# Stick-breaking attention with two keys to a scan step and a second projection with paired DMA transpositions

## Chip, cores and metric

The kernel runs on one core of one Trainium2 chip. The metric is the device time of one execution in microseconds (us); of several executions the median is taken. TensorE (PE in the profile) multiplies matrices, VectorE (DVE), ScalarE (ACT) and GpSimd (POOL) work element by element, SyncE (SP) issues most of the transfers.

## What is computed

Two transformer layers over 2048 tokens of width 1024. The change touches two pieces of the second layer. The first is the stick-breaking attention (4 heads of width 64, worked as 2 units of two heads), the second is the output projection with its residual and norm, which hands its rows to the feed-forward part.

```python
def stick_breaking_attention(q, k, v, g):
    ...
        z = jnp.einsum('bqhd,bkhd->bhqk', qb, kb).astype(jnp.float32) * scale
        mask = jnp.arange(end)[None, :] < (start + jnp.arange(Q_BLOCK))[:, None]
        log_1mb = jnp.where(mask, jax.nn.log_sigmoid(-z), 0.0)
        suffix = lax.cumsum(log_1mb, axis=3, reverse=True) - log_1mb
        a = jnp.where(mask, jnp.exp(jax.nn.log_sigmoid(z) + suffix), 0.0)
        outs.append(jnp.einsum('bhqk,bkhd->bqhd', a.astype(vb.dtype), vb))
    ...
    # second_block
        x = x + jnp.einsum('bse,ed->bsd', mix, w_out[l])
        h2 = rmsnorm(x, norm2_g[l])
        gate = jnp.einsum('bsd,df->bsf', h2, w_gate[l])
        up = jnp.einsum('bsd,df->bsf', h2, w_up[l])
        x = x + jnp.einsum('bsf,fd->bsd', jax.nn.silu(gate) * up, w_down[l])
```

## The kernel before

The program is built by a scheduler that sets the order on each engine by its own estimate, within what the data allow; each engine then works its list strictly in that order. Every f32 operand of a large product is kept as a sum of two f16 parts, a high part (a cast on ACT) and a low part (the difference, on POOL or DVE).

The span falls into five stretches: the first layer (0 to about 985 us), the attention of the second layer (`block2`, about 985 to 1950), its output projection (`out2`, overlapped with the end of the attention, to about 2110), the first half of the feed-forward part (`ffn_in`, to about 2970) and its second half (`ffn_out`).

`block2` works six units in turn; two of them are stick-breaking units (`stick`, from about 990 and from about 1456 us), four are differential-attention units (`diff`). The q, k, v projections of the following work (`unit_gemm`, tile `pg`) are mixed between the rows of a unit. In a stick unit each of 16 query blocks i has (i + 1) * 128 keys and two heads r; a row of keys is cut in pieces of at most 1024, the last keys first. That makes 48 pieces and 34,816 keys per partition and unit. A piece (`piece`, L1012) goes:

- scores on PE into PSUM (tile `sc`, four banks, L892 to L895);
- one minus beta as a sigmoid on ACT, PSUM to SBUF tile `e` (`g` in the code, six buffers, L1016);
- for the diagonal block beta itself, a second sigmoid on ACT, in place in PSUM (L1019);
- on DVE the running product over the keys from the last to the first, one key a step, in place (L1021), started from the first key of the piece before it (`carry`);
- on DVE the product of the last 127 keys with beta, read from PSUM (L1025);
- in `parts` the f16 high part on ACT (L907), the low part on POOL (L910), then one DMA transposition on SP (L912);
- some pieces later the sum over the values on PE (L922, L923).

The value rows are replaced by differences of neighbouring rows beforehand, so that the running product itself, and beta in the diagonal block alone, stand in for the attention weights. The delay between a piece and its parts is set by `self.pipe`: its split comes one piece later, its sum three more.

`out2` runs eight steps `u` of two token tiles each: load y and the residual x1 (SP), 48 matmuls per tile into `pq` (L665 to L667), add to the residual on DVE (L668), sum of squares on ACT into a junk PSUM bank (L670), store of x to `x2d` from SP (L671), the norm on DVE (L674, which overwrites x and so waits for that store), sums for a Strassen-like scheme (`seven`), high and low parts (L681, L682), and the DMA transpositions of those parts into the seven tiles `T7` (L693). The parts of one step are four of high and four of low; the low ones lie across the pairs in `T7`, so three of them take two transpositions each: eleven in a step. All of SP's transfers are issued in one list.

Of the kernel before, what the change touches and what calls it, by code (L numbers as in the profile page):

```python
# [7 lines left out]
F32 = mybir.dt.float32  # L8
# [3 lines left out]
AF = mybir.ActivationFunctionType  # L12
ALU = mybir.AluOpType
AX = mybir.AxisListType
PSUM = bass.MemoryType.PSUM
# [25 lines left out]
UN = (3, 6, 4, 4)  # L41
LAST_B = 2
PIPE = 2
UNITS = (0, 2, 3, 1, 4, 5)
MIX_ROWS = (0, 2)
FF = 2816
# [20 lines left out]
class Kernel:  # L67
# [556 lines left out]
    def out2(self, cw):  # L624

        nc, a = self.nc, self.a
        sm = self.pool("usm", 4, ctx=cw)  # L630
        gen = self.pool("gen", 3, ctx=cw)
        yp = self.pool("uy", 8, ctx=cw)
        m = self.pool("um", 5, ctx=cw)
        hp = self.pool("uh", 5, ctx=cw)
        sp = self.pool("us", 1, ctx=cw)
        pq = self.banks("upq", UPQ, cw)
        jp = self.pool("ujk", 1, PSUM, ctx=cw)
        w = [self.row_weight(a["wo2"], k, None if k < 5 else gen) for k in range(KD)]
        self.x2d = [self.dram.tile([128, 2, D], F32, name=f"x2d{t}") for t in range(8)]
        slots = [(self.x7, "x7")] * 6 + [(self.tp, "th")] * 4 + [(self.tp, "tl")] * 4  # L640
        self.T7 = [
            [pool.tile([128, 4, 2, 512], F16, tag=tag, name=tag) for pool, tag in slots[7 * h:7 * h + 7]]
            for h in range(2)
        ]
        gr = self.bcast(self.ws, a["n2"], D, "ws")
        for u in range(4 * NB // 2):
            half, tp = u // 4, u % 4
            xs = []
            for q in range(2):
                y = []  # L650
                for p in range(2):
                    t = yp.tile([128, KD, 128], F16, tag="y", name="y")
                    nc.sync.dma_start(t, self.y2d[2 * half + q][p][:, tp])
                    y.append(t)
                yh, yl = y
                r = m.tile([128, 2, 512], F32, tag="x2", name="x2")
                rf = r.rearrange("p h n -> p (h n)")
                nc.sync.dma_start(rf, self.x1d[8 * half + 4 * q + tp])
                ss = sm.tile([128, 2], F32, tag="ss", name="ss")
                for n in range(2):  # L660
                    ns = slice(n * 512, (n + 1) * 512)
                    ps = pq()
                    for k in range(KD):
                        wh, wl = w[k]
                        nc.tensor.matmul(ps, yh[:, k], wh[:, ns], start=k == 0, stop=False)  # L665
                        nc.tensor.matmul(ps, yh[:, k], wl[:, ns], start=False, stop=False)
                        nc.tensor.matmul(ps, yl[:, k], wh[:, ns], start=False, stop=k == KD - 1)  # L667
                    nc.vector.tensor_tensor(r[:, n], r[:, n], ps, ALU.add)  # L668
                    junk = jp.tile([128, 512], F32, tag="junk", name="junk")
                    nc.scalar.activation(junk, r[:, n], AF.Square, accum_out=ss[:, n:n + 1])  # L670
                nc.sync.dma_start(self.x2d[u][:, q], rf)  # L671
                nc.gpsimd.tensor_tensor(ss[:, 0:1], ss[:, 0:1], ss[:, 1:2], ALU.add)
                self.rstd(ss[:, 0:1], ss[:, 0:1], self.eps_rms, 1.0 / D)
                nc.vector.scalar_tensor_tensor(rf, rf, ss[:, 0:1], gr, ALU.mult, ALU.mult)  # L674
                xs.append(r)
            s3 = sp.tile([128, 3, 512], F32, tag="s3", name="s3")
            self.seven(xs[0], xs[1], *[s3[:, j] for j in range(3)], nc.vector)
            for j, src in enumerate((xs[0], xs[1], s3[:, 0:2], s3[:, 2:3])):
                n = src.shape[1]
                hl = [hp.tile([128, 2, 512], F16, tag="hl", name="hl")[:, 0:n] for _ in range(2)]  # L680
                nc.scalar.copy(hl[0], src)  # L681
                nc.vector.tensor_tensor(hl[1], src, hl[0], ALU.subtract)  # L682
                for p in range(2):
                    i = 7 * p + 2 * j
                    if n == 2 and i % 2 == 0:
                        spots = [(self.T7[half][i // 2][:, tp], hl[p])]
                    else:
                        spots = [
                            (self.T7[half][(i + x) // 2][:, tp, (i + x) % 2:(i + x) % 2 + 1], hl[p][:, x:x + 1])
                            for x in range(n)  # L690
                        ]
                    for to, of in spots:
                        nc.sync.dma_start_transpose(  # L693
                            to.rearrange("p x (k t) -> p (x k) t", t=128), of.rearrange("p x n -> p (x n)")
                        )

    def seven(self, r1, r2, s1, s2, s4, eng=None):

# [7 lines left out]
    def block2(self):  # L706
        self.y2d = self.y_scratch("y2d")
        with ExitStack() as c2:
# [3 lines left out]
            self.yp = self.pool("ayp", 1, ctx=c2)  # L712
            self.one = self.pool("aone", 1, ctx=c2)
            self.sm = self.pool("asm", 4, ctx=c2)
            self.pg = self.pool("pg", PGN, PSUM, ctx=c2)
            self.sc = self.pool("sc", SCN, PSUM, ctx=c2)
            self.po = self.pool("apo", PON, PSUM, ctx=c2)
# [2 lines left out]
            units += [("diff", 2 + h, 2 + h, 6 + h, 10 + h) for h in range(4)]  # L720
            units = [units[j] for j in UNITS]
            gemms = [self.unit_gemm(w, kind == "sb") for kind, _, *w in units]
            self.turn = self.turn2 = 0
            self.pipe, self.mixed = [], []
            self.later = []
            made = [0] * len(units) + [3 * NB]
            due = 0
# [276 lines left out]
    def stick(self, ops, k, b):  # L1004

        nc = self.nc
        rows = {}  # L1010

        def piece(i, r, p0, n, carry):  # L1012
            g = self.etile(0)
            own = None
            for ps, p, w in reversed(self.scores(ops, r, i, True, p0, p0 + n)):
                nc.scalar.activation(g[:, p - p0:p - p0 + w], ps[:, 0:w], AF.Sigmoid, scale=-1.0)  # L1016
                if p + w == (i + 1) * 128:
                    own = ps[:, w - 128:w - 1]
                    nc.scalar.activation(own, own, AF.Sigmoid)  # L1019
            rev = g[:, 0:n][:, ::-1]  # L1020
            nc.vector.tensor_tensor_scan(  # L1021
                rev, rev, self.zero.to_broadcast([128, n]), 1.0 if carry is None else carry, ALU.mult, ALU.add
            )
            if own is not None:
                nc.vector.tensor_tensor(g[:, n - 127:n], g[:, n - 127:n], own, ALU.mult)  # L1025

            def split():
                t = self.parts([(g[:, 0:n], 0, n)], g, self.etile(1), n, nc.gpsimd, True)
                self.pipe.append((PIPE, lambda: sum_up(t)))

            def sum_up(t):
                c = i % 4
                if r == 0 and carry is None:
                    rows[i] = self.po.tile([128, 2, 128], F32, tag="po", name="po")
                    if c == 0:
                        rows["o8"] = self.m.tile([128, 4, 2, 128], F32, tag="o4", name="o8")
                cols = slice(r * 64, (r + 1) * 64)
                self.spread(
                    [(t, p0 // 128, n // 128)], ops, cols, rows[i][:, :, cols], i, carry is None, p0 == 0
                )  # L1040
                if r == 1 and p0 == 0:
                    nc.vector.tensor_copy(rows["o8"][:, c], rows[i])
                    if c == 3:
                        ended()

            self.pipe.append((1, split))
            return g[:, 0:1] if p0 else None

        def ended():
            o4 = self.summed(rows["o8"])  # L1050

            def done():
                self.head_norm(o4, 64)
                self.finish(o4, k, b, self.col("sg"))

            self.later.append((LAST_DELAY if self.last_unit else DELAY, done))

        for c in range(4):
            i = b * 4 + c
            W = (i + 1) * 128  # L1060
            for r in range(2):
                carry = None
                for p0 in reversed(range(0, W, PIECE)):
                    carry = piece(i, r, p0, min(PIECE, W - p0), carry)
                    self.step()
            yield
        if b == NB - 1:
            while self.pipe:
                self.step()
# [44 lines left out]
        self.store(self.y2d, ct, b, ps, self.col("pscale", ct))  # L1114

    def part(self, half, p, q):
        i = 7 * p + q
        return self.T7[half][i // 2][:, :, i % 2]

    def ffn(self):  # L1120

# [315 lines left out]
```

## Time and profile before

| what | value |
|---|---|
| median of 3 runs | 3392.9 us (3389.72 to 3398.15) |
| profiled execution, its own time | 3387.5 us |
| its span, first to last instruction | 3385.7 us |
| PE busy | 3114.2 us (92%) |
| DVE busy | 2209.4 us (65%) |
| POOL busy | 1419.8 us (42%) |
| ACT busy | 1241.9 us (37%) |
| mean granted clock of PE | 0.967 of full speed |

The profile gives each engine's busy time, its instructions by source line with the operand names (out<-in), and the idle time of an engine with what ended it. A DVE or POOL duration includes time in which the instruction waits inside the engine. Busy times by stretch show which engine sets the pace where.

### The profile page before, as it was taken

How to read it: one execution, taken by the hardware profiler on the slowest of the kernel's cores; microseconds unless marked ns; L12 is line 12 of the kernel's file. 1: busy time of each engine (PE TensorE's matmuls, PEld its weight loads, DVE VectorE, ACT ScalarE, POOL GpSimd, SP SyncE). 2: the span in 40 equal slices, each digit the busy share in tenths (PEclk: the TensorE clock that was granted, in tenths of full speed). 3: DMA queues.
4: the chain of work that ended last, by engine and by line, in shares of the span. 5: the costliest groups of instructions: out<-in, count | busy, mean ns of one | idle time of the engine just before them, and what ended most of it. 6: DMA issues, size and time to landing. Idle time of an engine off the chain costs nothing. (4 is left out here: it accounts for less than half of the span.)

```text
span 3385.7 us, 46832 instructions
## 1 busy us (share of the span) xinstructions
PE 3114.2 (92%) x17736; PEld 1584.8 (47%) x17736; DVE 2209.4 (65%) x3573; ACT 1241.9 (37%) x2371; POOL 1419.8 (42%) x1155
## 2 busy tenths in 40 slices
PE   8999998999987798987798898899999999999998
PEld 4454454785434454544445443344444444334443
DVE  6986979624658886678856754456555655754437
ACT  5233232322136565565546632323222332311103
POOL 5344344413348644368734421333222233344324
PEclk9999999999989899999899999999999999999999
DMA  5101021214767764577556778322222222454334
GB/s 191 33 21 48 13 51 44 55 48 148 198 154 143 144 130 94 121 138 139 107 111 125 185 177 194 105 81 69 97 69 69 84 81 81 170 184 135 111 101 168
DMA packets 605570, 373.93 MB, mean 110 GB/s; under 512 B 508320, under 2 KB 549024, under 8 KB 604320
## 3 DMA queue, kind: packets, MB, share of 16 engines
q1 hardware_dynamic: 560192, 338.78, 39.1%
q10 hardware_dynamic: 45152, 32.17, 3.3%
q8 instruction: 139, 2.28, 0.3%
q14 instruction: 87, 0.71, 0.1%
HBM read 162.70 MB, written 82.31 MB: 72 GB/s over the span
## 5 line engine op out<-in xcount | busy, mean ns | idle before, releaser
L144 PE MATMUL pg<-th,w 128*128 128x512 f16 x1344 | 518.1, 386 | 24.8 <-DVE r L592 10.3
L146 PE MATMUL pg<-th,w 128*128 128x512 f16 x1344 | 519.7, 387 | 6.4 <-POOL w L123 3.2
L145 PE MATMUL pg<-tl,w 128*128 128x512 f16 x1344 | 519.2, 386 | 0.7 <-DVE tl L183 0.7
L910 POOL TENSOR_TENSOR e<-e 128x1024 f16<-128x1024 f32 (+7 forms) x192 | 366.7, 1925 | 231.2 <-ACT e L907 189.8
L1021 DVE TENSOR_TENSOR_SCAN e<-e,few 128x128 f32<-128x128 f32 (+7 forms) x96 | 223.7, 2347 | 36.1 <-ACT e L1016 24.0
L892 PE MATMUL sc<-k,q 128*128 128x512 f16 (+3 forms) x480 | 173.4, 364 | 63.1 <-DVE e L1025 44.2
L922 PE MATMUL po<-v,e 128*128 128x256 f16 (+1 forms) x1024 | 165.5, 264 | 66.5 <-DMA e<-e 62.8
L1161 POOL TENSOR_TENSOR w<-ws,w 128x1024 f16<-128x1024 f32 x20 | 48.6, 2431 | 393.2 <-ACT w L1160 393.2
L144 PEld LDWEIGHTS <-w 128*128 128x128 f16 x1344 | 133.6, 99 | 167.8 <-ACT w L122 13.7
L907 ACT CAST e<-e 128x1024 f16<-128x1024 f32 (+7 forms) x192 | 150.6, 794 | 167.1 <-DVE e L968 53.4
L145 PEld LDWEIGHTS <-w 128*128 128x128 f16 x1344 | 133.6, 99 | 166.6 <-issue 27.3
L146 PEld LDWEIGHTS <-w 128*128 128x128 f16 x1344 | 133.5, 99 | 163.8 <-issue 11.6
L1193 PEld LDWEIGHTS <-w 128*128 128x128 f16 x1232 | 121.1, 98 | 172.3 <-issue 32.6
L953 ACT ACTIVATE e<-e,nm 128x1024 f32<-128x1024 f32 (+4 forms) x192 | 171.2, 892 | 67.1 <-DVE e L948 50.0
L467 DVE SCALAR_TENSOR_TENSOR acc<-h,cols,acc 128x512 f32<-128x512 f32 x240 | 193.3, 825 | 2.4
L1192 PEld LDWEIGHTS <-w 128*128 128x128 f16 x1232 | 121.2, 98 | 155.7 <-ACT w L1160 8.7
L1194 PEld LDWEIGHTS <-w 128*128 128x128 f16 x1232 | 121.2, 98 | 150.3 <-issue 3.9
L893 PE MATMUL sc<-k,q 128*128 128x512 f16 (+3 forms) x480 | 172.8, 364 | 0.0
L123 POOL TENSOR_TENSOR w<-ws,w 128x1024 f16<-128x1024 f32 x52 | 117.7, 2266 | 125.2 <-ACT w L122 125.2
L922 PEld LDWEIGHTS <-e 128*128 128x128 f16 x1088 | 109.8, 105 | 108.2 <-DMA e<-e 75.2
L923 PE MATMUL po<-v,e 128*128 128x128 f16 (+1 forms) x1024 | 157.9, 218 | 0.0
L948 DVE TENSOR_SCALAR_CACHE_REDUCE e<-sc,nm 128x512 f32<-128x512 f32 (+3 forms) x192 | 123.0, 647 | 32.4 <-PE sc L893 12.9
(327 smaller groups left out, 7861.6 us busy)
## 6 DMA issues: line engine op xcount, KB each, us to landing
mid<-md SPq DMA_DIRECT2D x88, 448.0 KB, 4.2
ws<-in_w SPq DMA_DIRECT2D x48, 512.0 KB, 3.7
md<-mid SPq DMA_DIRECT2D x44, 512.0 KB, 3.4
md<-mid SPq DMA_DIRECT2D x22, 768.0 KB, 5.3
q<-qn SPq DMA_DIRECT2D x96, 128.0 KB, 2.6
ws<-in_wg SPq DMA_DIRECT2D x22, 512.0 KB, 3.5
ws<-in_wu SPq DMA_DIRECT2D x22, 512.0 KB, 4.1
ws<-in_wd SPq DMA_DIRECT2D x22, 512.0 KB, 4.3
```

Of the source, the lines that this page charges most:

```text
L144: nc.tensor.matmul(ps, wh[:, k], th[:, k], start=k == 0, stop=False)
L145: nc.tensor.matmul(ps, wh[:, k], tl[:, k], start=False, stop=False)
L146: nc.tensor.matmul(ps, wl[:, k], th[:, k], start=False, stop=k == KD - 1)
L467: nc.vector.scalar_tensor_tensor(acc[:, ct], src, wcol, acc[:, ct], ALU.mult, ALU.add)
L892: nc.tensor.matmul(ps[:, 0:n], q[:, 0], kk, start=True, stop=False)
L893: nc.tensor.matmul(ps[:, 0:n], q[:, 1], kk, start=False, stop=not last)
L907: cast = nc.scalar.copy(fv[:, o:o + w], src)
L910: eng.tensor_tensor(fv[:, n + o:n + o + w], src, fv[:, o:o + w], ALU.subtract)
L922: nc.tensor.matmul(po, t[:, 0, j], v, start=first and x == 0, stop=False)
L923: nc.tensor.matmul(po[:, 0], t[:, 1, j], v[:, 0], start=False, stop=last and x == len(todo) - 1)
L953: nc.scalar.activation(e[r][:, 0:n], e[r][:, 0:n], AF.Exp, bias=nm[:, len(sc) - 1:len(sc)], scale=-1.0, accum_out=ss[:, r, x:x + 1])
L1021: nc.vector.tensor_tensor_scan(rev, rev, self.zero.to_broadcast([128, n]), 1.0 if carry is None else carry, ALU.mult, ALU.add)
```

## The change

In a stick unit a scan step takes two keys: the recurrence multiplies by the odd and by the even key and writes the even position; the odd positions are then multiplied by their neighbour in a separate DVE instruction of half the piece. A piece that continues another first copies the carry behind its last key. Beta of the diagonal block goes to SBUF (tile `own`, three buffers), and its product moves to GpSimd. The low part of every third piece is made on VectorE. In `out2` the low parts get their own pairs of `T7` slots, so that each part is one transposition, eight in a step; the store to `x2d` is issued from ScalarE; the junk bank is taken from the other end of PSUM.

```diff
+LO_SHARE = 3
...
-        jp = self.pool("ujk", 1, PSUM, ctx=cw)
+        jp = self.pool("ujk", 1, PSUM, ctx=cw, side="right")
...
-                nc.sync.dma_start(self.x2d[u][:, q], rf)
+                nc.scalar.dma_start(self.x2d[u][:, q], rf)
...
                 for p in range(2):
-                    i = 7 * p + 2 * j
-                    if n == 2 and i % 2 == 0:
-                        spots = [(self.T7[half][i // 2][:, tp], hl[p])]
-                    else:
-                        spots = [
-                            (self.T7[half][(i + x) // 2][:, tp, (i + x) % 2:(i + x) % 2 + 1], hl[p][:, x:x + 1])
-                            for x in range(n)
-                        ]
-                    for to, of in spots:
-                        nc.sync.dma_start_transpose(
-                            to.rearrange("p x (k t) -> p (x k) t", t=128), of.rearrange("p x n -> p (x n)")
-                        )
+                    at = self.spot(p, 2 * j)
+                    nc.sync.dma_start_transpose(
+                        self.T7[half][at // 2][:, tp, at % 2:at % 2 + n].rearrange("p x (k t) -> p (x k) t", t=128),
+                        hl[p].rearrange("p x n -> p (x n)"),
+                    )
+
+    def spot(self, p, q):
+
+        return q if p == 0 else 8 + q if q < 6 else 7
...
+            self.bp = self.pool("abp", 3, ctx=c2)
...
                 if p + w == (i + 1) * 128:
-                    own = ps[:, w - 128:w - 1]
-                    nc.scalar.activation(own, own, AF.Sigmoid)
-            rev = g[:, 0:n][:, ::-1]
+                    own = self.bp.tile([128, 127], F32, tag="own", name="own")
+                    nc.scalar.activation(own, ps[:, w - 128:w - 1], AF.Sigmoid)
+            if carry is not None:
+                nc.vector.tensor_copy(g[:, n:n + 1], carry)
+            even, odd = [g[:, 0:n].rearrange("p (j x) -> p j x", x=2)[:, :, x] for x in range(2)]
             nc.vector.tensor_tensor_scan(
-                rev, rev, self.zero.to_broadcast([128, n]), 1.0 if carry is None else carry, ALU.mult, ALU.add
+                even[:, ::-1], odd[:, ::-1], even[:, ::-1], 1.0 if carry is None else carry, ALU.mult, ALU.mult
             )
+            w = n // 2 - (carry is None)
+            after = g[:, 2:n + 2].rearrange("p (j x) -> p j x", x=2)[:, 0:w, 0]
+            nc.vector.tensor_tensor(odd[:, 0:w], odd[:, 0:w], after, ALU.mult)
             if own is not None:
-                nc.vector.tensor_tensor(g[:, n - 127:n], g[:, n - 127:n], own, ALU.mult)
+                nc.gpsimd.tensor_tensor(g[:, n - 127:n], g[:, n - 127:n], own, ALU.mult)
+
+            self.pieces += 1
+            eng = nc.gpsimd if self.pieces % LO_SHARE else nc.vector
 
             def split():
-                t = self.parts([(g[:, 0:n], 0, n)], g, self.etile(1), n, nc.gpsimd, True)
+                t = self.parts([(g[:, 0:n], 0, n)], g, self.etile(1), n, eng, True)
...
     def part(self, half, p, q):
-        i = 7 * p + q
-        return self.T7[half][i // 2][:, :, i % 2]
+        at = self.spot(p, q)
+        return self.T7[half][at // 2][:, :, at % 2]
```

The scheduler moves instructions with it. On POOL, in the first stick unit at query block 12, the list before has low parts alone (the numbers are tile names; two pieces of each head alternate):

```order
L910 TENSOR_TENSOR e_10120<-e_10010,e_10120 128x1024
L910 TENSOR_TENSOR e_10150<-e_10098,e_10150 128x640
L910 TENSOR_TENSOR e_10175<-e_10124,e_10175 128x1024
L910 TENSOR_TENSOR e_10207<-e_10154,e_10207 128x640
L985 TENSOR_TENSOR o8_9689<-o8_9689 128x4x128
```

and after the change, at the same block, the products with beta (L1030) between them, and two of the low parts gone to DVE:

```order
L1030 TENSOR_TENSOR e_10165<-e_10165,own_10174 128x127
L909 TENSOR_TENSOR e_10189<-e_10075,e_10189 128x1024
L1030 TENSOR_TENSOR e_10225<-e_10225,own_10234 128x127
L909 TENSOR_TENSOR e_10248<-e_10193,e_10248 128x1024
L909 TENSOR_TENSOR e_10282<-e_10225,e_10282 128x640
L984 TENSOR_TENSOR o8_9734<-o8_9734 128x4x128
```

The product of the following diagonal piece (e_10225) now stands ahead of the low part of the piece before it (e_10193). On ACT at the same place after the change (L1016 and L1019 the sigmoids, L906 the casts):

```order
L1016 ACTIVATE e_10193<-sc_10197 128x512
L1016 ACTIVATE e_10225<-sc_10226 128x512
L1016 ACTIVATE e_10225<-sc_10229 128x128
L1019 ACTIVATE own_10234<-sc_10229 128x127
L1016 ACTIVATE e_10252<-sc_10253 128x512
L906 CAST e_10248<-e_10193 128x1024
L1016 ACTIVATE e_10252<-sc_10256 128x512
L906 CAST e_10282<-e_10225 128x640
```

A piece's cast stands behind the sigmoids of the next piece and ahead of those of the one after it, as it did before the change; what is new is that the cast of a diagonal piece (e_10225) now waits for POOL's product and not for DVE's.

On SP, in `out2`, step 6 of eight had these rows before (L671 stores to x2d):

```order
L671 DMA x2d6_18883<-x2_19981 128x1024
L693 DMA_TRANSPOSE th_18892<-hl_20050 128x8x128
L693 DMA_TRANSPOSE tl_18895<-hl_20051 128x4x128
L693 DMA_TRANSPOSE tl_18896<-hl_20051 128x4x128
L693 DMA_TRANSPOSE th_18893<-hl_20057 128x8x128
L693 DMA_TRANSPOSE th_18894<-hl_20064 128x8x128
L693 DMA_TRANSPOSE tl_18896<-hl_20058 128x4x128
L693 DMA_TRANSPOSE tl_18897<-hl_20058 128x4x128
L693 DMA_TRANSPOSE tl_18897<-hl_20065 128x4x128
L693 DMA_TRANSPOSE tl_18898<-hl_20065 128x4x128
L693 DMA_TRANSPOSE tl_18895<-hl_20071 128x4x128
L693 DMA_TRANSPOSE tl_18898<-hl_20072 128x4x128
```

and has these after it:

```order
L686 DMA_TRANSPOSE th_19088<-hl_20228 128x8x128
L686 DMA_TRANSPOSE tl_19092<-hl_20229 128x8x128
L659 DMA x2_20324<-x1d15_7508 128x1024
L686 DMA_TRANSPOSE th_19089<-hl_20234 128x8x128
L686 DMA_TRANSPOSE th_19090<-hl_20240 128x8x128
L686 DMA_TRANSPOSE tl_19093<-hl_20235 128x8x128
L686 DMA_TRANSPOSE tl_19094<-hl_20241 128x8x128
L686 DMA_TRANSPOSE tl_19091<-hl_20246 128x4x128
L686 DMA_TRANSPOSE tl_19091<-hl_20247 128x4x128
```

The three split pairs are whole, and the stores have left the list: they now stand in ACT's, right behind the second sum of squares of their tile.

## Rows read from the trace of the kernel before

**Rows 1.** The page's first part: busy us, share of the span and instructions by engine.

```profile
PE 3114.2 (92%) x17736; PEld 1584.8 (47%) x17736; DVE 2209.4 (65%) x3573; ACT 1241.9 (37%) x2371; POOL 1419.8 (42%) x1155
```

**Rows 2.** Busy us by stretch: both stick units, then two pieces of out2 and its end.

```profile
core 0: us, PE busy (x) PEld busy (x) DVE busy (x) ACT busy (x) POOL busy (x), PEclk, DMA share, GB/s
990.00:1169.00 179.00, 139.47 (x1026) 74.98 (x1025) 143.96 (x122) 101.38 (x237) 133.49 (x66) 0.93 0.72 141
1456.00:1642.00 186.00, 143.69 (x1038) 80.91 (x1037) 150.90 (x131) 109.84 (x251) 153.32 (x75) 0.88 0.72 134
...
2000.00:2050.00 50.00, 40.89 (x181) 17.63 (x178) 26.03 (x31) 13.83 (x25) 6.31 (x12) 0.92 0.89 227
2100.00:2140.00 40.00, 23.05 (x76) 8.19 (x75) 24.74 (x27) 15.02 (x22) 9.43 (x10) 0.79 0.66 155
```

**Rows 3.** DVE in order of time, first stick unit: start us, duration us, instruction [idle before].

```profile
992.77 0.42 DVE L1021 TENSOR_TENSOR_SCAN e<-e,few 128x128 f32<-128x128 f32 x1 [2.32 <-ACT e L1016]
...
1157.35 0.29 DVE L1025 TENSOR_TENSOR e<-e,sc 128x127 f32<-128x127 f32 x1
1157.56 2.35 DVE L1021 TENSOR_TENSOR_SCAN e<-e,few 128x1024 f32<-128x1024 f32 x1
...
1161.61 2.36 DVE L1021 TENSOR_TENSOR_SCAN e<-e,few 128x1024 f32<-128x1024 f32 x1 [1.71 <-issue]
...
1164.08 3.96 DVE L1021 TENSOR_TENSOR_SCAN e<-e,few 128x1024 f32<-128x1024 f32 x1
...
1168.80 0.14 DVE L962 COPY s<-ss 128x1 f32<-128x1 f32 x1
```

**Rows 4.** POOL in order of time, first stick unit.

```profile
995.55 0.43 POOL L910 TENSOR_TENSOR e<-e 128x128 f16<-128x128 f32 x1 [3.09 <-ACT e L907]
...
1111.36 2.12 POOL L910 TENSOR_TENSOR e<-e 128x1024 f16<-128x1024 f32 x1 [3.35 <-ACT e L907]
...
1158.85 7.04 POOL L910 TENSOR_TENSOR e<-e 128x1024 f16<-128x1024 f32 x2 [3.78 <-issue]
```

**Rows 5.** Waits in the second stick unit: us in total, times, longest.

```profile
PE sc L892 <- DVE e L1025: 29.1, 12, 5.1
...
ACT e L1016 <- PE po L923: 16.4, 11, 2.9
```

**Rows 6.** DVE in order of time at the end of out2.

```profile
2099.32 1.23 DVE L682 TENSOR_TENSOR hl<-x,hl 128x1024 f16<-128x1024 f32 x1 [1.11 <-ACT hl L681]
...
2118.37 2.50 DVE L674 SCALAR_TENSOR_TENSOR x<-x,ss,ws 128x1024 f32<-128x1024 f32 x2 [7.15 <-DMA x2d<-x]
```

**Rows 7.** First layer, line L385, 128 elements: runs of four or more (nt), single elements (f); min/median/max ns.

```profile
L385 DVE TENSOR_TENSOR Q<-Q,nt x96: 273/282/2211, 41.9 to 641.6; 128x128 f32<-128x128 f32 x96
L385 DVE TENSOR_TENSOR Q<-Q,f x48: 374/614/2343, 33.1 to 626.5; 128x128 f32<-128x128 f32 x48
```

**Rows 8.** SP's list in out2 by line, min/median/max ns; a third of the transpositions.

```profile
L693 SPq DMA_TRANSPOSE x<-hl x36: 1205/1258/2130, 1967.1 to 2040.6; - x36
...
L671 SPq DMA_DIRECT2D x2d<-x x16: 319/532/867, 1928.9 to 2116.0; - x16
```

**Rows 9.** PE in order of time in out2 and after: the matmuls with idle time before them.

```profile
2009.85 0.39 PE L665 MATMUL pq<-w,y 128*128 128x512 f16 x1 [2.08 <-DMA y<-y2d2h]
...
2051.45 0.61 PE L665 MATMUL pq<-w,y 128*128 128x512 f16 x1 [8.44 <-DMA y<-y2d3h]
...
2112.08 0.58 PE L1192 MATMUL pa<-x,w 128*128 128x512 f16 x1 [6.61 <-ACT junk L670]
2121.27 0.58 PE L1192 MATMUL pa<-x,w 128*128 128x512 f16 x1 [3.98 <-ACT s L1207]
2129.18 0.61 PE L1192 MATMUL pc<-x,w 128*128 128x512 f16 x1 [3.88 <-ACT w L1160]
```

**Rows 10.** SP in order of time at the end of out2.

```profile
2115.30 1.05 SPq L671 DMA_DIRECT2D x2d<-x  x2
...
2122.08 0.53 SPq L1148 DMA_DIRECT2D ws<-in_wg  x1
```

More of the change, by code (lines that the diff above doesn't have):

```diff
@@ L723, in block2 @@
             self.turn = self.turn2 = 0
-            self.pipe, self.mixed = [], []
+            self.pipe, self.mixed, self.pieces = [], [], 0
             self.later = []
```

## Prediction

> **What bounds the kernel now.** Read the page's busy shares first: PE is busy 92% of the span and no other engine over 65% [rows 1]. So an edit pays where PE stands idle, and nowhere else; 3385.7 - 3114.2 = 271.5 us are there to win. The busy times by stretch say where they lie. In the two stick units PE works 139.5 of 179 us and 143.7 of 186, so 40 and 42 us are idle; in out2 it is idle 9 of the 50 us from 2000 and 17 of the 40 from 2100 [rows 2]. These are the places that the change touches.
>
> What holds PE in the stick units? Neither DVE nor POOL alone is full (144 and 133 of 179 us), but the single rows show that they hinder each other. A scan of 1024 keys takes 2.35 us when POOL is quiet and 3.96 us when it is not; a low part takes 2.12 us alone, and two of them 7.04 us where scans run [rows 3, 4]. Follow those: from 1157.56 to 1168.04 us there lie three scans and two low parts, 3 x 2.36 + 2 x 2.12 = 11.3 us of undisturbed time in 10.5 us of wall time. The two engines work there almost as one; some (11.3 - 10.5) / 5 = 0.17 us of each instruction overlap with the other engine, and no more. PE sees it as waits for a score bank that the product with beta has not freed, 29.1 us in the second unit [rows 5]. So the pace of a stick unit is set by the **sum** of DVE's scans and POOL's low parts, and a term is worth what it takes from that sum.
>
> In out2 PE waits for y transfers (2.08 and 8.44 us) that stand in SP's list behind transpositions, and at its end for the junk bank, for a copy on ACT, and for the next weights (6.61, 3.98 and 3.88 us) [rows 9].
>
> **The change part by part, for one stick unit** (48 pieces, 34,816 keys). Two rows give the price of a scan: 0.42 us at 128 keys and 2.36 at 1024, so 2.17 ns a key and 0.14 us fixed [rows 3]. Likewise 1.89 ns and 0.19 us for a low part on POOL [rows 4], and, from 0.29 us at 127 elements and 1.23 at 1024, 1.05 ns and 0.16 us for a two-input instruction on DVE [rows 3, 6].
> - Scan: 48 x 0.14 + 34,816 x 2.17 ns = 82.3 us before; with half the steps 44.6. That a step of two multiplications costs what one of a multiplication and an addition does is an assumption.
> - Added, the product of the odd keys: 48 x 0.16 + 17,408 x 1.05 ns = 25.7 us. Scan and product together save 12.0.
> - Added, the copy of the carry: 16 x 0.14 = 2.2 us of DVE [rows 3], beside POOL's work; counted at nothing, at most 2.2.
> - A third of the low parts (16 of them, 12,288 keys): 26.2 us leave POOL, 15.4 come to DVE; 10.8 saved.
> - Beta's product: 32 x 0.29 = 9.3 us leave DVE, where its second operand came from PSUM; on POOL it takes what a low part of 128 does, 32 x 0.43 = 13.8 us, and these join the sum. Behind it in POOL's list stand low parts, and ACT's cast waits for it.
>
> The sum changes by -12.0 - 10.8 + 13.8 = -9.0 us. But there are now 176 instructions in it instead of 96 (scans, products, low parts, beta), and if each hides 0.17 us as the rows above do, 80 x 0.17 = 13.6 us more are hidden: -22.6. Between these ends I take the middle, -16, times 0.8, since the two engines together are busy only 77 and 82% of their time in the stretches [rows 2] and a saving counts only where they are full: **-13 us a unit, -26 for both**.
>
> The Trainium skill says otherwise of that overlap: by the page "SBUF — State Buffer", section "Who interferes with whom", a VectorE instruction with two SBUF inputs and a GpSimd instruction that reads SBUF exclude each other for the whole instruction. By that nothing of the added instructions would be hidden, and the sum would be -9; the rows agree on the exclusion and not on "whole" (0.17 us of each overlap).
>
> The new instructions read and write every second f32. In the first layer an instruction over single elements far apart takes 374 ns at best where one over runs takes 273 [rows 7]: (374 - 273) / 128 = 0.8 ns an element. If that held here, the product would cost 17,408 x 0.8 ns = 14 us more a unit; the scan's step of 2.17 ns has room for it. I take no surcharge, as an element out of each two lies nearer to runs than to elements 44 bytes apart, and keep the 14 for the range.
>
> **Out2.** Three transpositions a step fall away, 24 x 1.26 = 30 us of SP's list, and 16 stores of 0.53 us leave it, 8.5 more [rows 8]. ACT takes the stores; its list has room (13.8 busy of 50 us [rows 2]), and they stand behind a sum of squares that needs the same data, so nothing new waits. So y comes earlier: of the 10.5 us of PE's waits for y I take 9. At the end the last norm waits 7.15 us, from 2111.2 on, for stores that SP issues at 2115.30; the second half of the first gate weights goes out at 2122.08, since its buffer (`ws`) holds the norm's factors until that norm is done [rows 6, 10]. From ACT the last store starts right behind the square that follows at 2111.2, which I estimate to be 3 us earlier than 2115.30, and no transposition need be ahead of them; so those weights, which end PE's wait at 2129.18, come some 4 us earlier. The junk bank no longer coincides with the first bank of the feed-forward part, and the copy on ACT that PE waits for at 2121.27 now stands ahead of the casts. The three waits are 14.5 us in all; since the weights come last and only 4 us earlier, I take 5. Ends: 0 to 14.5 here, 0 to 10.5 for y. **Out2: -14 us.** Late next: the weights themselves.
>
> **Sum:** -26 - 14 = -40 us. Against the profiled execution's 3387.5 us that is 3347.5; the median of the runs is 5.4 us higher (3392.9), so the forecast for the median is **3353 us**. Units of diff, the first layer and the feed-forward loops are untouched; the scheduler keeps their order but for small swaps, taken at nothing (at most the 0.3%, 10 us, that a measurement of this kernel can tell from no change).
>
> **The rivals,** all against 3392.9.
> - *Whole exclusion.* The two engines hide nothing of the added instructions: 2 x -9 x 0.8 = -14, with out2's -14: 3365. For it: nothing but the rule above; against it: rows 3 and 4. Chance 0.15.
> - *Everything pays.* The sum falls by 22.6 a unit, PE's idle time in the units (82 us) gives way, and all of out2's waits go: -45 - 25 = 3323. For it: PE's gaps are that large. Chance 0.12.
> - *The stick units don't gain.* ACT's sigmoid already waits for PE to free one of six `e` buffers, 16.4 us in the second unit [rows 5]; beta's product on POOL lengthens a piece's way, and the buffers set the pace in place of the sum: only out2's -14, 3379. Chance 0.10.
> - *Nothing arrives.* PE's idle time only moves: y is late for the reordered loads, and the buffers as above: 3392. Chance 0.05.
> - *Slower: beta's product closes a loop.* ACT's list has a diagonal piece's cast ahead of the sigmoids of the piece two further on, and the cast now waits for POOL, where the product stands in line. The loop is cast 0.9, sigmoids 1.2, scan 1.2, product 0.7, beta 0.4 = 4.4 us for two pieces, against 186 / 48 x 2 = 7.8 now (the first two are estimates from the 100 us that ACT spends on 48 pieces [rows 2]). It decides once beta's product waits over 3.4 us a time: two low parts ahead of it, stretched as the pair of 7.04 us is, make 4.4 + 7.0 = 11.4 us, hence (11.4 - 7.8) / 2 = 1.8 us a piece; on a third of the 64 diagonal pieces + 38, with out2 + 24: 3417. Against it: the list shows one low part between two products, not two. A scan whose step cannot be halved, the change not doing what it says, would add 2 x 0.8 x 37.7 = 60 to the forecast and end near the same place. Chance of either 0.08.
>
> **How the numbers follow.** Forecast 0.50, rivals 0.15, 0.12, 0.10, 0.05, 0.08. Faster by over 0.3% means under 3382.7: the forecast, the first two rivals and 0.07 of the third, 0.84; within 0.3%: 0.08; slower by over 0.3%: 0.08. The range goes from *everything pays* (3322) to just past *the stick units don't gain* (3384), which leaves out the last two rivals and little else.
>
> **What would show it.** Right: scans of 1024 keys at 1.2 to 2 us and one product of 0.66 us or more beside each; PE's waits for DVE's product gone from the list of waits; stick units of some 166 and 173 us by stretch; in out2 64 transpositions, no wait of PE for y over 3 us, none for the junk bank. Wrong: scans still over 2.3 us; products far above 0.7 us where POOL is quiet (the step of two costs); stick units as long as before with ACT waiting for PE's `po`, or with casts waiting for POOL's L1030; PE idle elsewhere by what it saved here.

## The result and the profile after

The changed kernel takes **3348.8 us** (median of 4 runs, 3346.3 to 3356.4) beside 3394.8 for the kernel before in the same runs: a ratio of 0.9868, 95% interval 0.985 to 0.9886. The forecast was 3353, in a range from 3322 to 3384. The two traces differ by less, 31.2 us of span (3385.7 and 3354.5): the profiled execution of the kernel after was the longest of its four, that of before lay below all of its four. What the other 15 us are made of is in no trace.

The line of busy times on the page, to be held against [rows 1]:

```profile
PE 3098.5 (92%) x17736; PEld 1576.9 (47%) x17736; DVE 2203.8 (66%) x3669; ACT 1236.4 (37%) x2371; POOL 1360.0 (41%) x1187
```

PE's idle time fell from 271.5 to 256.0 us and its busy time by 15.7 for the same number of matmuls, at a mean granted clock of 0.970 in place of 0.967. That split is not to be relied on: in a second trace of the changed kernel (c0, below; span 3354.8 us) PE is busy 3108.6 us and idle 246.2, at 0.966.

Busy times by stretch, the same four places as in [rows 2] (PE, PEld, DVE, ACT, POOL with counts, granted clock, DMA share, GB/s):

```profile
988.00:1157.00 169.00, 137.76 (x1036) 75.04 (x1035) 140.28 (x174) 102.90 (x243) 107.16 (x84) 0.95 0.77 151
1440.00:1621.00 181.00, 139.48 (x1052) 77.68 (x1049) 153.81 (x182) 109.33 (x256) 127.33 (x95) 0.89 0.70 138
1979.00:2029.00 50.00, 45.75 (x200) 19.81 (x199) 28.09 (x34) 16.20 (x29) 5.48 (x12) 0.93 0.96 243
2070.00:2110.00 40.00, 19.60 (x60) 6.67 (x59) 25.74 (x25) 15.74 (x22) 9.15 (x10) 0.70 0.66 161
```

POOL lost 26 us in each stick unit; DVE is as busy as before. From the first to the last scan the units last 160.1 and 177.1 us in place of 171.3 and 183.0. In out2 the piece where PE waited for y has 4 idle us in place of 9, but its end is worse: 20 of 40 us idle, before 17.

DVE in order of time, end of the first unit (start us, duration us, instruction, idle time before; L1023 is the scan, L1028 the product of the odd keys, L909 the low part, L1021 the copy of the carry), and POOL over the same time (L1030 is the product with beta):

```profile
1144.25 1.75 DVE L1023 TENSOR_TENSOR_SCAN e<-e 128x512 f32<-128x512 f32 x1
1146.04 0.69 DVE L1028 TENSOR_TENSOR e<-e 128x512 f32<-128x512 f32 x1
1146.65 1.22 DVE L909 TENSOR_TENSOR e<-e 128x1024 f16<-128x1024 f32 x1
1147.78 1.22 DVE L1023 TENSOR_TENSOR_SCAN e<-e 128x512 f32<-128x512 f32 x1
1149.03 2.43 DVE L1028 TENSOR_TENSOR e<-e 128x511 f32<-128x511 f32 x1
```

```profile
1142.34 0.45 POOL L1030 TENSOR_TENSOR e<-e,own 128x127 f32<-128x127 f32 x1 [1.30 <-DVE e L1028]
1142.80 2.12 POOL L909 TENSOR_TENSOR e<-e 128x1024 f16<-128x1024 f32 x1
1147.94 2.98 POOL L909 TENSOR_TENSOR e<-e 128x1024 f16<-128x1024 f32 x1 [3.02 <-DVE e L909]
```

Undisturbed, a scan of 512 steps takes 1.22 us and a product of 512 elements 0.69. Beside POOL's low part of 1147.94 the product takes 2.43: the exclusion of [rows 3, 4] is as it was. It lengthens the instruction that begins second: the scan of 1147.78 keeps its 1.22 us although POOL's low part begins inside it, and that low part takes 2.98 us in place of 2.12.

The waits between 1441 and 1618 us, second unit (total us, times, longest):

```profile
ACT e L906 <- POOL e L1030: 25.7, 18, 3.6
PE po L921 <- DMA e<-e: 23.0, 15, 3.7
...
DVE e L1023 <- ACT e L1016: 16.1, 12, 4.3
...
ACT e L906 <- DVE e L1028: 14.0, 8, 4.4
...
ACT e L1016 <- PE po L922: 11.0, 3, 7.6
```

PE's wait for DVE's product, 29.1 us in [rows 5], is gone. PE now waits for transposed parts, and ACT's cast (L906) waits 39.7 us for the product of the odd keys and for beta.

PE's waits in and behind out2 (1840 to 2110 us), against [rows 9]:

```profile
PE pa L1200 <- ACT w L1168: 7.3, 1, 7.3
...
PE pc L1200 <- ACT w L1168: 5.1, 1, 5.1
PE pa L1202 <- DVE w L1169: 4.5, 1, 4.5
PE pq L666 <- DMA y<-y2d3h: 4.2, 1, 4.2
PE pc L1202 <- DVE w L1169: 2.8, 1, 2.8
...
PE pa L1200 <- ACT s L1215: 0.7, 1, 0.7
```

y: 4.2 us in place of 10.5. The junk bank: no wait. But the waits for the gate weights' casts have come in its place, 20.4 us in all at the end, where the three rows of before made 14.5 (17.0 with four smaller waits).

### The profile page after: what moved, and what is told of

The parts are those of the page before. It is cut to its first block, busy times and chain, and to the rows that moved or that the text cites. A ratio compares the mean times of both kernels' runs of the same rounds, so it can differ in the third digit from the quotient of the medians.

```text
span 3354.5 us, 46912 instructions
## 1 busy us (share of the span) xinstructions
PE 3098.5 (92%) x17736; PEld 1576.9 (47%) x17736; DVE 2203.8 (66%) x3669; ACT 1236.4 (37%) x2371; POOL 1360.0 (41%) x1187
## 5 line engine op out<-in xcount | busy, mean ns | idle before, releaser
L145 PE MATMUL pg<-th,w 128*128 128x512 f16 x1344 | 517.3, 385 | 25.4 <-DVE r L593 10.3
L909 POOL TENSOR_TENSOR e<-e 128x1024 f16<-128x1024 f32 (+7 forms) x160 | 268.4, 1687 | 209.2 <-ACT e L906 178.7
L145 PEld LDWEIGHTS <-w 128*128 128x128 f16 x1344 | 133.2, 99 | 168.0 <-ACT w L123 13.8
L147 PEld LDWEIGHTS <-w 128*128 128x128 f16 x1344 | 133.2, 99 | 163.6 <-issue 10.3
L906 ACT CAST e<-e 128x1024 f16<-128x1024 f32 (+7 forms) x192 | 150.6, 796 | 150.5 <-DVE e L967 56.3
L891 PE MATMUL sc<-k,q 128*128 128x512 f16 (+3 forms) x480 | 170.8, 358 | 30.8 <-DVE e L947 15.7
L952 ACT ACTIVATE e<-e,nm 128x1024 f32<-128x1024 f32 (+4 forms) x192 | 171.2, 892 | 72.7 <-DVE e L947 55.5
L1023 DVE TENSOR_TENSOR_SCAN e<-e 128x64 f32<-128x64 f32 (+7 forms) x96 | 116.7, 1224 | 30.5 <-ACT e L1016 30.4
```

Of the source, the lines that this page charges most:

```text
L145: nc.tensor.matmul(ps, wh[:, k], th[:, k], start=k == 0, stop=False)
L147: nc.tensor.matmul(ps, wl[:, k], th[:, k], start=False, stop=k == KD - 1)
L891: nc.tensor.matmul(ps[:, 0:n], q[:, 0], kk, start=True, stop=False)
L906: cast = nc.scalar.copy(fv[:, o:o + w], src)
L909: eng.tensor_tensor(fv[:, n + o:n + o + w], src, fv[:, o:o + w], ALU.subtract)
L952: nc.scalar.activation(e[r][:, 0:n], e[r][:, 0:n], AF.Exp, bias=nm[:, len(sc) - 1:len(sc)], scale=-1.0, accum_out=ss[:, r, x:x + 1])
```

## The experiments

Each run stands against the kernel before on the same chip. The changed kernel ran a second time as c0, beside e5, e6 and e8:

> The changed kernel once more, unchanged, as the base on this chip for the runs beside it: 3343 to 3356 us, ratio 0.985 to 0.989.

Measured: 3350.0 us, 0.9872. For the table three things were worked out from the traces, first unit and second, from first to last scan. *Sum*: every scan, two-input product and low part on DVE with both operands in SBUF, and all of POOL, each at the shortest duration that its shape has in that trace. *Either*: time in which at least one of them ran. *Cast*: ACT's idle time before its casts, whatever ended it, with the part that the profile puts down to issue. *PE idle* goes by the same two stretches. Each trace is of one execution, and not always of the median one: those of the changed kernel and of c0 are the longest of their four (7.5 and 6.6 us above the median), that of e10 is the shortest of its four, and that of e7 the longest of its six. e8 leaves the product of the odd keys out and so does not compute the attention.

| run | ratio to before, 95% | sum | either | cast | PE idle |
|---|---|---|---|---|---|
| before | 1 | 168.0 / 179.5 | 156.9 / 171.2 | 52.0 / 48.7 | 36.4 / 42.3 |
| changed | 0.9868 (0.985-0.9886) | 158.8 / 171.0 | 141.7 / 155.3 | 42.1 / 41.6 | 29.7 / 39.9 |
| changed, again (c0) | 0.9872 (0.9858-0.9885) | 158.9 / 171.1 | 142.0 / 155.4 | 38.3 / 41.6 | 28.6 / 39.9 |
| e1 out2 alone | 0.9965 (0.9953-0.9978) | as before | as before | 50.9 / 48.7 | 36.5 / 42.2 |
| e2 stick alone | 0.9914 (0.9901-0.9928) | as changed | as changed | 42.2 / 40.9 | 30.0 / 35.9 |
| e7 scan back | 0.9917 (0.9897-0.9936) | 171.1 / 182.7 | 158.8 / 170.6 | 50.8 / 53.9 | 34.9 / 42.3 |
| e5 low on POOL | 0.9877 (0.9863-0.989) | 169.9 / 180.5 | 154.1 / 165.8 | 42.6 / 42.9 | 25.1 / 41.8 |
| e6 half on DVE | 0.9827 (0.9809-0.9844) | 153.9 / 164.6 | 138.8 / 149.8 | 45.7 / 39.6 | 26.8 / 34.4 |
| e4 beta on DVE | 0.9889 (0.9874-0.9904) | 153.3 / 169.7 | 139.3 / 156.3 | 47.8 / 54.9 | 29.7 / 44.9 |
| e8 no product | 0.9816 (0.9803-0.983) | 135.5 / 147.0 | 125.2 / 140.6 | 32.5 / 33.8 | 22.3 / 33.8 |
| e10 cast later | 0.9828 (0.9815-0.9841) | 160.0 / 172.3 | 143.9 / 157.5 | 12.2 / 25.2 | 14.4 / 34.7 |
| f3 half, cast later | 0.9834 (0.9821-0.9848) | 152.3 / 167.0 | 136.4 / 152.4 | 15.6 / 24.4 | 17.7 / 33.9 |

**The two halves apart (e1, e2).** e1 takes the `out2` hunks of the diff alone, e2 all the others.

> The kernel before with the second projection's part of the change alone (paired transpositions and the new places, stores from ACT, junk bank on the other side). By the prediction's term: 14 us faster than before (y 9, end 5). By the trace of after, in which PE's wait for y fell from 10.5 to 4.2 us but the waits at the end grew from 14.5 to about 20: 0 to 7 us faster, with PE's longest wait at the end for the weights' cast and the norms on DVE waiting some 4 us each for the stores. If this part does nothing at all: within 3 us of before.

> The changed kernel with the second projection put back: the stick part of the change alone. By the sum of the instructions that exclude each other: 26 us faster than before by the prediction, 24 by the place of the last score matmul in the trace of after (1897.9 against 1921.9). If exclusion were whole, 14 faster. If the out2 part carried the gain: under 10 faster.

Measured: e1 3382.6 us, 10.3 faster than before (medians); e2 3364.5, 28.4 faster. 0.0035 + 0.0086 = 0.0121, and both together give 0.0130: the halves add up. In e1's trace the end of out2 looks as in the kernel after:

```profile
PE pc L1189 <- ACT w L1157: 6.2, 1, 6.2
PE pa L1189 <- ACT w L1157: 6.1, 1, 6.1
...
PE pa L1191 <- DVE w L1158: 4.5, 1, 4.5
PE pq L665 <- DMA y<-y2d3h: 3.3, 1, 3.3
```

e2's has the old ones again:

```profile
PE pq L666 <- DMA y<-y2d3h: 10.2, 1, 10.2
PE pa L1203 <- ACT junk L671: 8.5, 1, 8.5
...
PE pa L1203 <- ACT s L1218: 3.9, 1, 3.9
PE pc L1203 <- ACT w L1171: 3.5, 1, 3.5
```

So this half saves the wait for y and exchanges the junk bank for the weights.

**Why the weights are late (e3).** DVE in order of time at the end of out2, kernel after (L669 the add, L675 the norm):

```profile
2079.14 0.68 DVE L669 TENSOR_TENSOR x<-x,pq 128x512 f32<-128x512 f32 x1
2084.18 1.28 DVE L675 SCALAR_TENSOR_TENSOR x<-x,ss,ws 128x1024 f32<-128x1024 f32 x1 [4.36 <-DMA x2d<-x]
2085.38 0.68 DVE L669 TENSOR_TENSOR x<-x,pq 128x512 f32<-128x512 f32 x1
...
2088.25 0.68 DVE L669 TENSOR_TENSOR x<-x,pq 128x512 f32<-128x512 f32 x1
2093.16 1.28 DVE L675 SCALAR_TENSOR_TENSOR x<-x,ss,ws 128x1024 f32<-128x1024 f32 x1 [4.23 <-DMA x2d<-x]
```

Each norm waits over 4 us for the store of the x that it overwrites, and the next tile's adds stand behind it. In [rows 6] two norms shared one wait of 7.15 us. The last norm frees the buffer of the second gate weights:

```profile
2094.47 0.35 SPq L1156 DMA_DIRECT2D ws<-in_wg  x1
```

That is 20.9 us after the last `pq` group began (2073.6), where the kernel before took 17.4 (2122.08 [rows 10], 2104.7). e3 gives the norm a place of its own:

```diff
-        m = self.pool("um", 5, ctx=cw)
+        m = self.pool("um", 3, ctx=cw)
+        xp = self.pool("uxn", 2, ctx=cw)
...
-                nc.vector.scalar_tensor_tensor(rf, rf, ss[:, 0:1], gr, ALU.mult, ALU.mult)
-                xs.append(r)
+                xn = xp.tile([128, 2, 512], F32, tag="xn", name="xn")
+                nc.vector.scalar_tensor_tensor(
+                    xn.rearrange("p h n -> p (h n)"), rf, ss[:, 0:1], gr, ALU.mult, ALU.mult
+                )
+                xs.append(xn)
```

> The changed kernel, the norm of the second projection written to a buffer of its own (three x2 buffers and two for the norm in place of five). Theory A (the norms wait for the x2d stores since they write in place, 4.2 to 5 us each at the end, and the last adds and the second gate weights stand behind them on DVE): those waits go, PE's 20 us of waits at the end fall to 12 or less, 8 to 12 us faster than the changed kernel. Theory B (the weights are late for SP's list or POOL's chain, and the norms only fill the time): within 3 us of the changed kernel, the waits for the weights' cast still 5 us and more.

The norms now wait 2.02 us for their factor, and the weights leave at 2087.57, 14.1 us after the last `pq` group began (2073.5) in place of 20.9:

```profile
2083.55 0.68 DVE L670 TENSOR_TENSOR x<-x,pq 128x512 f32<-128x512 f32 x1
2086.26 1.29 DVE L677 SCALAR_TENSOR_TENSOR xn<-x,ss,ws 128x1024 f32<-128x1024 f32 x1 [2.02 <-POOL ss L190]
```

PE's waits at the end fell to 13.7 us (6.9 + 3.3 + 1.8 + 1.0 + 0.7), while the wait for y rose to 7.3 with two x2 buffers fewer. So the weights are late for the reason that Theory A gives, but its gain of 8 us or more in time is not there: the runs' ratio is 0.9866 (0.9853 to 0.988), which is Theory B's figure, and on top of e6 (f1, below) it gave nothing either. The trace is 6.2 us shorter because the profiled execution of the changed kernel lay 7.5 us above its median and that of e3 only 1.5.

**Is the sum the pace of a stick unit? (e4, e5, e6, e8).** The edits, in that order, each alone: `nc.vector` for `nc.gpsimd` in beta's product; `LO_SHARE = 1000`; `LO_SHARE = 2`; and

```diff
-            nc.vector.tensor_tensor(odd[:, 0:w], odd[:, 0:w], after, ALU.mult)
```

> The changed kernel with beta's product on DVE, both operands in SBUF as now. Theory A (sum of both engines): per unit 14.4 us leave POOL and 9.3 come to DVE, 5.1 less, times 0.8, two units: 8 us faster than the changed kernel, more if ACT's waits for that product (53.5 us in 38 waits) go as well. Theory B (DVE alone is the bound, POOL has room): 9.3 more on DVE, times 0.8, two units: 15 us slower.

> The changed kernel with all low parts of the stick units on POOL again (16 pieces a unit go back). Theory A (the sum of both engines sets the pace, as predicted): 26.2 us on POOL for 15.4 on DVE, 10.8 more a unit, times 0.8, two units: 17 us slower than the changed kernel. Theory B (DVE's list is the pace and POOL has room, as the run with beta's product on DVE suggests, 4 us slower where the sum said 8 faster): 15.4 us leave DVE in each unit: as fast or up to 20 us faster.

> The changed kernel with every second low part of the stick units on DVE instead of every third (8 pieces a unit more). Theory A (sum): 13 us leave POOL, 7.7 come to DVE, 5.4 less a unit, times 0.8, two units: 9 us faster than the changed kernel. Theory B (DVE's list is the pace): 7.7 more in each unit: up to 12 us slower.

> The changed kernel without the product of the odd keys, which is left out. Its 48 instructions a unit have 24.7 us alone and 42 to 47 us as they ran. Theory A (sum): 24.7 less 48 x 0.09 us that they hid = 20.4 a unit, times 0.8, two units: 33 us faster than the changed kernel. Theory B (DVE's list as it runs): up to 45 a unit until something else binds: 40 us or more faster. Theory C (PE's own work and the six e buffers bind by now, with PE busy 138 of 169 us): 15 us or less.

Measured: e4 3352.4 us, e5 3353.5, e6 3337.0, e8 3332.9; c0 3350.0 (3349.2 to 3356.6). No theory holds for all. Theory A fails with e5: 11.1 and 9.5 us more sum cost 3 us, which the intervals do not tell from nothing, and not 17. It fails with e4, which has less sum and is no faster. Theory B fails with e6, which has more on DVE and is 13 us faster. In e8, 23.3 and 24.0 us of sum gave 17, half of A's 33 and close to theory C's 15. The column of the casts does not order the four either (c0 shows that 4 us in a unit are scatter). The waits are longest with e4; in its second unit ACT's list shows them (1439 to 1623 us):

```profile
ACT e L906 <- DVE e L1030: 31.5, 15, 4.4
...
ACT e L906 <- DVE e L1028: 15.9, 8, 3.9
```

But e6 has 85.3 us of them in its two units, no less than the changed kernel (83.7, and 79.9 in c0), and is 13 us faster. In its first unit the profile puts a part of them down to issue (992.4 to 1151.3 us):

```profile
ACT e L906 <- POOL e L1030: 22.7, 17, 3.4
...
ACT e L906 <- issue: 16.4, 7, 3.1
...
ACT e L906 <- DVE e L1028: 6.7, 5, 3.4
```

Each of these seven ends within 0.16 us after a product of DVE (L1028), so they are waits like the others. Only about half of e6's gain lies here: from the first scan of the first stick unit to the last scan of the second the changed kernel takes 626.6 us (625.6 in c0) and e6 619.1. Why e6 is faster is open.

**The order on ACT (e10).** ACT in order of time, kernel after, second unit (L1016 and L1019 sigmoids, L906 the cast):

```profile
1515.65 0.30 ACT L906 CAST e<-e 128x128 f16<-128x128 f32 x1 [2.79 <-POOL e L1030]
...
1516.34 0.38 ACT L1016 ACTIVATE e<-sc 128x256 f32<-128x256 f32 x1
1516.60 0.28 ACT L1019 ACTIVATE own<-sc 128x127 f32<-128x127 f32 x1
1518.87 1.05 ACT L906 CAST e<-e 128x1024 f16<-128x1024 f32 x1 [1.99 <-DVE e L1028]
1519.82 0.59 ACT L1016 ACTIVATE e<-sc 128x512 f32<-128x512 f32 x1
```

The cast waits for POOL or DVE, and the next pieces' sigmoids stand behind it, so that later DVE has no scan to do. e10 moves each cast one piece back on the list, with the low part and the transposition that belong to it, and leaves the sums over V where they were:

```diff
-PIPE = 2
+PIPE = 1
...
-            self.pipe.append((1, split))
+            self.pipe.append((2, split))
```

> The changed kernel with each piece's cast one piece later on ACT, behind the sigmoids of the piece after the next, and the products with V at their old place (lag 2 and 1 in place of 1 and 2). Theory C (ACT's list is the loop: the cast waits 42 us in the second unit for the product and beta, and the sigmoids behind it wait with it, so that DVE's scans wait for ACT): those waits fall by half or more, 15 to 30 us faster than the changed kernel. Theory A (the sum of DVE and POOL): within 4 us. Theory E (PE's waits for the transposed parts, 25 us in that unit, bind, and they now come one piece later): 10 to 25 us slower.

Measured: 3334.1 us, 14 to 16 under the changed kernel, with the same instructions and nearly the same sum (160.0 and 172.3). The waits of its second unit (1428 to 1602 us):

```profile
ACT e L1016 <- PE po L922: 22.9, 16, 3.6
PE po L921 <- DMA e<-e: 15.9, 13, 4.2
ACT e L906 <- POOL e L1030: 15.3, 12, 2.9
...
ACT e L906 <- DVE e L1028: 9.9, 6, 3.2
...
DVE e L1023 <- ACT e L1016: 5.4, 7, 1.3
```

The casts' waits fell from 83.7 to 37.4 us in the two units, DVE's for ACT in the second from 16.1 to 5.4, and PE idles 14.4 us in the first unit in place of 29.7. From the first scan of the first unit to the last of the second the trace takes 610.7 us, 15 to 16 less than with the changed kernel. So the order is worth what theory C says, at the lower end of its 15 to 30; theory E is excluded, since PE's waits for transposed parts fell too. Whether it is the cast's place on ACT's list alone, or also the low part's on POOL's and DVE's, is not separated. What is late next are the `e` buffers: a sigmoid waits for PE to have used the old piece, 22.9 us in this unit.

**The scan by itself (e7)** goes back to one key a step:

```diff
-            if carry is not None:
-                nc.vector.tensor_copy(g[:, n:n + 1], carry)
...
+            rev = g[:, 0:n][:, ::-1]
             nc.vector.tensor_tensor_scan(
-                even[:, ::-1], odd[:, ::-1], even[:, ::-1], 1.0 if carry is None else carry, ALU.mult, ALU.mult
+                rev, rev, self.zero.to_broadcast([128, n]), 1.0 if carry is None else carry, ALU.mult, ALU.add
             )
...
-            nc.vector.tensor_tensor(odd[:, 0:w], odd[:, 0:w], after, ALU.mult)
```

> The changed kernel with the scan of one key a step again (no product of odd keys, no copy of the carry); low parts, beta and the second projection as changed. Theory A (sum): 79.5 us of scans in place of 42.5 + 24.7 in each unit, 12.3 more, and 48 instructions fewer that hide 0.09 us each, 16.6 in all, times 0.8, two units: 27 us slower than the changed kernel. Theory D (what is left when the other parts are taken off: low parts 3 us and beta's product within 4 of the 28 that the stick part brought): 20 to 28 slower. Theory C (the chain of one piece paces, not the sum; scan and product take 1.40 us a piece on the average, one scan 1.66): 0.26 us x 48 pieces x 2 units / 2 pieces in a loop: 12 slower.

Measured: 3369.4 us, wide (3351.4 to 3379.8); by the ratios 0.0045 of 3392, so 15 us slower than the changed kernel, by the medians 19. That is between C and D and short of A's 27. The scan is the larger part of the 28. The casts' waits are the longest of all runs, 50.8 and 53.9 us; the long scan stands ahead of each cast.

**Versions that beat both.** f1 is e6 with e3's norm, f3 is e6 with e10's order.

> Every second low part on DVE, and the norm of the second projection in buffers of its own, both on top of the changed kernel. If the gain of the former (13 to 15 us) stands and the latter stays worth nothing: 3335 us, ratio 0.983. If the latter's 6 us of PE waits, which its trace showed less, count beside it: 3329, ratio 0.981.

> The changed kernel with every second low part on DVE and the cast one piece later, the two edits that gained 13 to 15 us each alone. If they shorten the same waits (ACT's cast for POOL's and DVE's products): 3330 to 3336 us, ratio 0.982 to 0.983. If each takes its own share (POOL's list by the one, ACT's order by the other): 3320, ratio 0.979. If PE's six e buffers, for which ACT waited 22.9 us in the second unit with the cast later, bind both: 3333 with these waits at 25 us or more.

f1 3336.1 us, 0.9836 (0.9823 to 0.9848); f3 3335.4, 0.9834: nothing beyond e6 or e10 alone. f3's casts wait 40.0 us, no less than e10's 37.4, and its sigmoids 16.5 for the `e` buffers in the second unit. The two gains do not add; as e6 alone leaves the casts' waits as they are, that both shorten the same waits is not shown, nor that the buffers bind. By the ratios e6 (0.9827) and e10 (0.9828) are the best, and the intervals do not separate any of the four.

## Why the prediction was right, step by step

**Out2: -14 forecast, -10 measured (e1, -7.5 to -16).** y: 9 of 10.5 was taken, the trace shows 6.3. The end: 5 was taken for weights that come 4 us earlier; they came 3.5 later, and from the last `pq` group to the steady matmuls of the feed-forward part it is 38.5 us (2073.6 to 2112.1), before 37.6 (2104.7 to 2142.3). The step that failed is "From ACT the last store starts right behind the square": it does, at 2089.06, but that square is itself late, since the norm ahead of its add on DVE waits for a store of its own. A store that is issued early doesn't help a list that waits for every one of them.

**The prices in the stick units: right.** Scan and product were to save 12.0 us a unit; the scans' least durations fell from 79.5 to 42.5 and the products have 24.7: 12.3. The low parts take 15.0 us on DVE (forecast 15.4), beta's products 14.4 on POOL (13.8). The sum fell by 9.2 and 8.5 (forecast 9.0). The time in which either engine worked fell by 15.2 and 15.9 (forecast 16, the middle between 9.0 and 22.6), but in part for another reason. By the Trainium skill, page "SBUF — State Buffer", section "Who interferes with whom", it would have fallen by the sum alone; the trace has 6.0 and 7.4 us more. Of these, 2.2 and 2.5 us are successive records of one engine that overlap (on DVE by 0.08 us, as 1146.04 + 0.69 and 1146.65 in the rows above); so some 0.05 to 0.06 us of each of 80 added instructions lie beside the other engine, a third of the 0.17 that the rows of before gave. One of those rows was read loosely: POOL is not quiet beside the scan of 2.35 us, its pair of low parts begins inside it, at 1158.85. No surcharge for every second f32: the product of 512 elements takes 0.69 us, as L700 does over runs of 512.

**What the sum is worth: wrong.** The step that failed is "the pace of a stick unit is set by the **sum** [...] and a term is worth what it takes from that sum", with its factor of 0.8. By it the low parts on DVE bring 17 us; taken back they cost 3 (e5). By it beta on POOL costs 22 (13.8 x 0.8 x 2); putting it back on DVE, from SBUF, should gain 8 and gains nothing (e4, 3352 beside 3349 and 3350). Of the scan's 27 some 15 to 19 arrive (e7). If the parts add up, 6 to 10 of the 28 us are left for beta's move, a gain where the sum had a cost; it is also the part that took the product out of the score bank, for which PE had waited 29.1 us. No run shows it alone. Errors of opposite signs cancelled, so that -28 stands beside a forecast of -26 by luck.

What holds the pace in place of the sum is shown only in part. One thing is the loop that the text has as a rival for "slower": cast, sigmoids, scan, product, beta, cast. e10, which shortens the casts' waits, gains 14 to 16 us. The loop was there before the change (52.0 and 48.7 us of waits at the cast), and the change shortened its scan while it added a product and POOL's list to it (42.1 and 41.6). "Against it: the list shows one low part between two products" was enough against a loss, but left the loop without a price. It is not the whole: e6 gains 13 us and leaves these waits as they are.

**The rivals.** Whole exclusion (3365), no gain in the stick units (3379) and nothing arriving are excluded by e2, which is 24 to 34 us faster than before by its interval. Of the first one's mechanism more holds than was granted, though: of the 13.6 us that the added instructions of a unit were to hide, the traces have 3.8 and 4.9. Everything pays (3323) is excluded by PE's 29.7 and 39.9 idle us. That a scan's step could not be halved is excluded by its 1.22 us.

**The signs named beforehand.** Scans of 1.2 to 2 us for 1024 keys: right, the 20 of the second unit have a mean of 1.65. PE's waits for DVE's product: gone. Units of 166 and 173 us: 169 and 181 by the stretches shown, so the gain was less in the second unit and lay partly between the units. PE's wait for y under 3 us: 4.2. No wait for the junk bank: right, as are the 64 transpositions.

Not tried: beta in PSUM with its product on DVE, as before, under the new scan; so its own share of the 28 us is open. More `e` buffers weren't tried either, so whether they bind is open. Open too is where e3's 6.7 us of shorter waits at the end go: 3.1 came back in the wait for y, and the rest is less than the interval of its ratio can tell.

## What to carry over

Two engines that exclude each other make a good price list and a poor pace: before a sum is multiplied by a share, look for the in-order list that waits on both of them, here ACT's cast with the next pieces' sigmoids behind it, and try its order first, since e10 gained some 15 us with two numbers and no instruction changed. Count the idle time that a profile puts down to issue among the waits: without it e6's casts would seem to wait 23 us less than they do. An in-place update behind a store puts the store's latency on its engine, whoever issues the store. Undo each part of a change by itself even where the total comes out as forecast; here two of the terms were wrong.

## What was not expected of the hardware

A scan's price goes by its steps and not by what a step does or whether its operands lie 4 or 8 bytes apart. The shortest scan of 512 steps took 1.19 us in the trace of before (a multiplication and an addition over runs) and 1.19 in that of after (two multiplications over every second f32).

Also, PE's busy time is not fixed by its matmuls. The same 17,736 took 3098.5 us in one execution of the changed kernel, at a mean granted clock of 0.970, and 3108.6 in the other, at 0.966, and the spans differ by 0.3 us. From the kernel before to e6 the busy time fell from 3114.2 to 3087.3 us and the clock rose from 0.967 to 0.975, which is more than that; but that less waiting did it is not shown, for f3 idles less than e6 (231.4 and 247.9 us) and has 3099.4 us busy at 0.970.
